# Prompt attention moved beside the end of the attention input projection; sample heads alone in the attention loop, and both prompt output projections at its head

## The chip, the core and the metric

The kernel runs on one core of one Trainium2 chip. That core has TensorE (PE, the matrix multiplies), VectorE (DVE), ScalarE (ACT) and GpSimd (POOL), and SyncE (SP), whose queue issues nearly all transfers between HBM and the on-chip memory. The metric is the device time of one execution in microseconds (us). Everything is computed in float32 precision: each product is built from a rounded high half and a low rest, so that one product takes two or three matmuls.

## The reference

One step of a small diffusion backbone with two layers over 256 prompt tokens and 2048 sample tokens of width 1024. Layer 0 is a convolution branch, layer 1 an attention branch. Only layer 1 matters here:

```
q, k, v, z = split(h @ w_in, 4)                       # 1024 -> 4 x 1024, 16 heads of 64
prompt:  o = softmax(q k^T / 8) v                     # 256 x 256 per head, no mask
sample:  o = softmax([q k_loc^T/8 + bias, q k_ctx^T/8]) [v_loc; v_ctx]
         # k_loc: an 8 x 16 window of the 32 x 64 grid; k_ctx: 512 cached keys
x = x + gate * ((o * silu(z)) @ w_out)                # for prompt and sample, same weights, own gate
y = rms_norm(x) * final_g
```

The outputs are the normalised prompt and sample rows and the new k and v of the prompt. The prompt attention reads nothing that the sample attention makes, and the other way round.

## The kernel before

Phase 1 does the convolution layer and then the projections `w_in` of the attention layer, in two batches: first the prompt and the first 768 sample tokens (list A), later the other 1280 sample tokens (list B). `na_values` makes v, and `na_rest` makes k, z and q in 24 steps, one for each 128 columns of one of the three. A step of list B is 72 matmuls on PE. Every result goes to scratch in HBM (`ks_d`, `qh_d`, `ql_d`, `zn_d`, `vp_d`, `vs_d`), and the attention loads it from there. Instructions of a side list are woven between these steps: `weave(main, side, n)` takes n steps of the side for each step of the main work. The side list beside list B is `context_keys` (8 steps), `masked_bias` (48), `gated_weights` (32; it multiplies `w_out` with the gate and writes it to `w2_d`) and `context_values` (8). The Tile scheduler then sets the order of each engine in phase 1; in phase 2 the written order holds for PE and DVE, and the scheduler orders the other engines.

Phase 2 (`attention`) runs over units. A sample head of a group G of 512 tokens has four units of 128 queries, so 16 heads and 4 groups make 256 units; they come in two half-passes of 8 heads (`hg` 0 and 1, each over G = 0 to 3). One step i of the loop works on several units at once: scores of unit i (`sa_S`), minimum and bias on DVE, exponential on ACT, scaling on POOL, transposes on PE (`sa_T`), splitting in two halves on ACT and DVE (`sa_pt`), and the value product (`sa_O`). Prompt heads are units too: two heads form one unit (`pa_S`, `pa_T`, `pa_O`), and four such units stand at the head of each half-pass as G = None, before its sample heads. In the program text the names of the prompt's loaded tiles are `aNone_k`, `aNone_qh`, `aNone_ql`, `aNone_v` and `aNone_z`.

When a group has its heads done, `out_group` multiplies with half of `w2_d`, in chunks of six matmuls. `side_chunk` runs one chunk in every second step, as filling between the attention's own matmuls; if more than seven tiles would wait (`tiles_left`), `split` runs chunks at once until there is room, a burst. The weights are loaded by `load_w2`: four tiles of 128 x 4 x 512 numbers for one half-pass and one gate, of which the kernel holds one set. The first set is loaded at loop step 18 (`W2_STEP`), each next one as the set before it is finished with. All loads go through SP's queue in order; a load that waits for its buffer holds up all behind it.

```
for hg in range(2):
    ctx = {}
    for G in (None, 0, 1, 2, 3):
        grp = {"hg": hg, "G": G, "n": NPR if G is None else 512}
        self.sequence += [Head(grp, ctx, 8 * hg + i) for i in range(0, 8, 2 if G is None else 1)]
```

Of the kernel before, what the change touches and what calls it, by code (L numbers as in the profile page):

```python
# [11 lines left out]
F32 = mybir.dt.float32  # L12
# [3 lines left out]
ALU = mybir.AluOpType  # L16
# [32 lines left out]
BEGIN = 10  # L49
NEAR = 3  # L50
W2_STEP = 18
# [24 lines left out]
class Kern:  # L76
    def __init__(self, ctx, tc, io):
# [21 lines left out]
        self.rpb_d = d("rpb_d", [P + 1, RPB_PITCH])  # L99

# [941 lines left out]
    def masked_bias(self):  # L1042

        nc = self.nc
        work = lambda shape, tag, bufs, name: self.bp.tile(shape, F32, tag=tag, name=name, bufs=bufs)
# [119 lines left out]

    @staticmethod
    def weave(main, side, n):

        due = 0
        for _ in main:  # L1170
            due += n
            while due >= 1:
                next(side, None)
                due -= 1

    def phase1(self):
        tc = self.tc
        with ExitStack() as c:
# [19 lines left out]
            self.pc = extra.enter_context(tc.tile_pool(name="lnps", bufs=1, space=bass.MemoryType.PSUM))  # L1198
# [11 lines left out]
            side = itertools.chain(self.context_keys(), self.masked_bias(), self.gated_weights(), self.context_values())  # L1210
            rest = self.na_rest(B)
            with tc.tile_pool(name="bp", bufs=1, side="right") as self.bp:
                self.weave(self.na_values(B, lambda: next(rest)), side, 2)
                self.weave(itertools.islice(rest, 21), side, 3.5)
                for _ in side:
                    pass
# [6 lines left out]
    def start_attention(self):  # L1223
# [4 lines left out]
        for hg in range(2):  # L1228
            ctx = {}
            for G in (None, 0, 1, 2, 3):  # L1230
                grp = {"hg": hg, "G": G, "n": NPR if G is None else 512}
                self.sequence += [Head(grp, ctx, 8 * hg + i) for i in range(0, 8, 2 if G is None else 1)]
# [30 lines left out]
    def attention(self):  # L1263
# [3 lines left out]
        units = [(hd, j) for hd in heads for j in ([0] if hd.G is None else range(4))]  # L1267
# [6 lines left out]
        for i in range(-1, len(units) + 4):  # L1274
            self.step = i
            if i == W2_STEP:
                for h in range(2):
                    self.load_w2(0, 0, h, True)

            def go(u, new=False):  # L1280
# [3 lines left out]
                if new:  # L1284
                    if j == 0:
                        self.load_ahead(order[id(hd)] + 1)
                    gens[u] = self.prompt_unit(hd) if hd.G is None else self.sample_unit(hd, j)
# [9 lines left out]
            if 0 <= i - 3 < len(units):  # L1297
                hd, j = units[i - 3]
                if hd.G is None:
                    self.side_chunk()  # L1300
                    self.prompt_values(hd)
                elif j % 2:
# [33 lines left out]
    def load_head(self, hd):  # L1336
        nc, T, h, G, b = self.nc, self.T, hd.h, hd.G, hd.b
        nm = f"a{G}_{h}"
        a = 0 if G is None else NPR + G * 512
        n = hd.n  # L1340
        rows = slice(h // 2 * P, h // 2 * P + P)
        if G is None:
            hd.k = T("kt", [P, 2, NPR], F32R, nm + "_k")
            nc.sync.dma_start(hd.k.bitcast(F32), self.ks_d[h : h + 2, :, :, 0:NPR].rearrange("h s d t -> (s d) h t"))
            hd.q, hd.ql = (T(t, [P, 2, NPR], F32R, f"{nm}_{t}") for t in ("qh", "ql"))
            for t, d in ((hd.q, self.qh_d), (hd.ql, self.ql_d)):
                src = d[h * DH : h * DH + P, 0:NPR].rearrange("(e d) t -> d e t", e=2)
                for half in range(2):
                    nc.sync.dma_start(t[half * DH : half * DH + DH].bitcast(F32), src)
            hd.v = T("vl", [P, 2, 4, DH], F32R, nm + "_v")  # L1350
            nc.sync.dma_start(hd.v.bitcast(F32), self.vp_d[:, h : h + 2].rearrange("(u t) h s d -> t u (h s) d", t=P))
            hd.z = T("z", [P, n], F32, nm + "_z")
            nc.sync.dma_start(hd.z, self.zn_d[rows, a : a + n])
            return
# [42 lines left out]

    def prompt_unit(self, hd):

        nc, T = self.nc, self.T  # L1400
        nm = f"pa{hd.h}"
        S = self.bank("S", nm + "_S", 2, 1024)
        for e in range(2):
            for u in range(2):
                cs = slice(u * P, u * P + P)
                self.scores(S[:, (2 * e + u) * NPR : (2 * e + u + 1) * NPR], hd.q[:, e, cs], hd.ql[:, e, cs], hd.k[:, e])
        yield
        m = self.sm.tile([P, 8], F32, tag="m", name=nm + "_m")
        nc.vector.tensor_reduce(out=m[:, 0:4], in_=S.rearrange("p (x k) -> p x k", x=4), axis=AX.X, op=ALU.min)
        yield  # L1410
        p = T("p", [P, 4, NPR], F32, nm + "_p")
        for x in range(4):
            nc.scalar.activation(p[:, x], S[:, x * NPR : x * NPR + NPR], AF.Exp, scale=-1.0, bias=m[:, x : x + 1], accum_out=m[:, 4 + x : 5 + x])
        nc.vector.reciprocal(m[:, 4:8], m[:, 4:8])
        for x in range(4):
            nc.gpsimd.tensor_scalar(out=p[:, x], in0=p[:, x], scalar1=m[:, 4 + x : 5 + x], scalar2=1.0, op0=ALU.mult, op1=ALU.mult)
        yield
        ts = [self.bank("T", f"{nm}_T{e}", 2) for e in range(2)]
        for e, t in enumerate(ts):
            for u in range(2):  # L1420
                for kc in range(2):
                    nc.tensor.transpose(t[:, (2 * kc + u) * P : (2 * kc + u + 1) * P], p[:, 2 * e + u, kc * P : kc * P + P], self.ident)
        yield
        hd.pt = T("pt", [P, 2, 2, 2, NPR], F32R, nm + "_pt")
        flat = hd.pt.rearrange("p e s k q -> p e s (k q)")
# [289 lines left out]
```

## Time and profile before

| what | value |
|---|---|
| time, median of 3 runs | 2861.8 us (2847.99 to 2865.89) |
| time of the profiled execution | 2854.11 us |
| its span, first to last instruction | 2852.3 us |
| PE busy | 2706.4 us, 95% of the span |
| DVE, ACT, POOL busy | 1847.0, 1439.1, 1505.3 us |
| mean granted TensorE clock | 0.982 |
| DMA | 543.83 MB, mean 191 GB/s |

1.8 us of the profiled time lie outside its span. Times below are counted from the span's start. The last projection of phase 1 ends at about 1804 us and the last attention unit at about 2811 us; what follows is the last group's output projection. A row of the windows view gives a stretch, its length, the busy time of each engine in it with the number of its instructions, the granted clock of TensorE, the busy share of the DMA engines and what they moved. If a line is chosen, the busy time and the count are of that line alone: line L1465 is the reciprocal that each sample unit has once, so its count is the number of sample units in the stretch. L1607 is the third matmul of the output projection; a chunk has two of it. In a row of the timeline stand start, length, engine, line, operation, what is written and read, and in brackets how long the engine stood idle before it and what it waited for.

### The profile page before, as it was taken

How to read it: one execution, taken by the hardware profiler on the slowest of the kernel's cores; microseconds unless marked ns; L12 is line 12 of the kernel's file. 1: busy time of each engine (PE TensorE's matmuls, PEld its weight loads, DVE VectorE, ACT ScalarE, POOL GpSimd, SP SyncE). 2: the span in 40 equal slices, each digit the busy share in tenths (PEclk: the TensorE clock that was granted, in tenths of full speed). 3: DMA queues.
4: the chain of work that ended last, by engine and by line, in shares of the span. 5: the costliest groups of instructions: out<-in, count | busy, mean ns of one | idle time of the engine just before them, and what ended most of it. 6: DMA issues, size and time to landing. Idle time of an engine off the chain costs nothing.

```text
span 2852.3 us, 45385 instructions
## 1 busy us (share of the span) xinstructions
PE 2706.4 (95%) x16079; PEld 2340.2 (82%) x16079; DVE 1847.0 (65%) x3126; ACT 1439.1 (50%) x2538; POOL 1505.3 (53%) x1647
## 2 busy tenths in 40 slices
PE   6999999999899999999999999798999999999998
PEld 4888877776677889999988888687888888888887
DVE  4789989999876500023466530477778776888885
ACT  4457566676543312233222221466667665677774
POOL 4678878888554333355113331344555554556564
PEclk9999999999999999999999999899999999999999
DMA  7233555555435554447789984778776887976763
GB/s 253 87 122 111 190 170 161 185 192 178 148 114 167 161 158 128 121 149 237 238 297 356 339 283 128 195 199 224 202 197 186 212 219 200 248 211 184 199 169 108
DMA packets 429100, 543.83 MB, mean 191 GB/s; under 512 B 42562, under 2 KB 299674, under 8 KB 428745
## 3 DMA queue, kind: packets, MB, share of 16 engines
q1 hardware_dynamic: 423552, 517.97, 60.9%
q10 hardware_dynamic: 5320, 22.95, 2.1%
q8 instruction: 128, 2.10, 0.3%
q14 instruction: 100, 0.81, 0.1%
HBM read 357.76 MB, written 187.13 MB: 191 GB/s over the span
## 4 chain that ended last, share of the span: by engine, by line
PE 73%; DMA 9%; DVE 8%; ACT 4%; POOL 3%; issue 2%; SPq 2%; POOLq 0%; ACTq 0%; DVEq 0%
PE sa_T L1472 7%; PE ni_s L350 6%; PE ni_s L351 6%; PE ni_s L349 6%; PE ci_ps L349 5%; PE ci_ps L350 5%; PE ci_ps L351 5%; PE sa_O L1501 5%; PE sa_O L1496 4%; PE sa_S L1395 3%; PE sa_S L1394 3%; DVE cv L500 2%; PE o L1605 2%; PE o L1607 2%; PE o L1606 2%
## 5 line engine op out<-in xcount | busy, mean ns | idle before, releaser
L1466 POOL TENSOR_SCALAR sa_p<-sa_p,sa_m 128x992 f32<-128x992 f32 (+2 forms) x256 | 279.5, 1092 | 430.4 <-DVE sa_m L1465 307.1
L500 DVE SCALAR_TENSOR_TENSOR cv<-u,dw,cv 128x640 f32<-128x640 f32 (+2 forms) x570 | 427.8, 822 | 3.8 <-ACT cv L496 2.9
L1481 ACT CAST sa_pt<-sa_T 128x512 fp32r<-128x512 f32 (+3 forms) x512 | 275.6, 588 | 228.2 <-PE sa_T L1472 226.5
L109 DVE TENSOR_TENSOR sa_pt<-sa_T,sa_pt 128x512 fp32r<-128x512 f32 (+3 forms) x512 | 328.6, 682 | 3.1 <-ACT sa_pt L1481 2.5
L349 PE MATMUL ci_ps<-h_s_hi,ci_wh 128*128 128x512 f32 x768 | 307.2, 400 | 2.0 <-DVE shift L237 1.0
L351 PE MATMUL ci_ps<-h_s_hi,ci_wl 128*128 128x512 f32 x768 | 303.0, 395 | 0.0
L350 PE MATMUL ci_ps<-h_s_lo,ci_wh 128*128 128x512 f32 x768 | 302.8, 394 | 0.0
L1464 ACT ACTIVATE sa_p<-sa_S,sa_m 128x992 f32<-128x992 f32 (+2 forms) x256 | 267.2, 1044 | 64.4 <-DVE sa_m L1460 52.1
L1472 PE MATMUL sa_T<-ident,sa_p 128*128 128x128 f32 (+3 forms) x2048 | 273.7, 277 | 18.9 <-DVE sa_pt L109 18.4
L1472 PEld LDWEIGHTS sa_T<-ident,sa_p 128*128 128x128 f32 (+3 forms) x2048 | 240.2, 138 | 53.7 <-POOL None_y1l L106 14.2
L1458 DVE TENSOR_REDUCE sa_m<-sa_S 128x1 f32<-128x512 f32 x256 | 176.2, 688 | 161.3 <-PE sa_S L1395 145.0
L481 POOL TENSOR_TENSOR cv_s<-cv_s,cv_p 128x519 f32<-128x519 f32 (+1 forms) x155 | 233.1, 1504 | 69.7 <-DVE cv_s L504 49.0
L478 ACT ACTIVATE cv_p<-u,dw 128x640 f32<-128x640 f32 (+2 forms) x326 | 240.9, 770 | 54.4 <-POOL cv_s L481 35.7
L481 POOL TENSOR_TENSOR cv_p<-cv_p,cv_p 128x520 f32<-128x520 f32 (+1 forms) x155 | 227.7, 1469 | 26.6 <-ACT cv_p L478 18.9
L1501 PE MATMUL sa_O<-sa_pt,a_v 120*128 120x256 f32 (+5 forms) x1280 | 192.6, 281 | 0.0
L1496 PE MATMUL sa_O<-sa_pt,cv 128*128 128x256 f32 x1024 | 177.3, 296 | 2.9 <-ACT sa_pt L1481 1.4
L349 PEld LDWEIGHTS ci_ps<-h_s_hi,ci_wh 128*128 128x128 f32 x768 | 145.2, 189 | 39.1 <-ACT cv_p L478 2.5
L1460 DVE CUSTOM_DVE_ANT_0 sa_S<-sa_S,a_bm,sa_m 128x480 f32<-128x480 f32 (+2 forms) x256 | 170.9, 668 | 9.0
L351 PEld LDWEIGHTS ci_ps<-h_s_hi,ci_wl 128*128 128x128 f32 x768 | 145.1, 189 | 33.8
L350 PEld LDWEIGHTS ci_ps<-h_s_lo,ci_wh 128*128 128x128 f32 x768 | 145.5, 189 | 31.0
L1501 PEld LDWEIGHTS sa_O<-sa_pt,a_v 120*128 120x128 f32 (+2 forms) x1280 | 169.5, 193 | 0.0
L106 POOL TENSOR_TENSOR nis_wl<-nis_w,nis_wh 128x1024 fp32r<-128x1024 f32 x24 | 58.6, 2446 | 187.1 <-ACT nis_wh L341 159.0
(843 smaller groups left out, 7265.1 us busy)
## 6 DMA issues: line engine op xcount, KB each, us to landing
adaw<-in_ada_w SPq DMA_DIRECT2D x24, 1024.0 KB
ci_w<-in_conv_w_in SPq DMA_DIRECT2D x48, 512.0 KB
a_bm<-bm_d SPq DMA_DIRECT2D x32, 720.0 KB
x_s<-in_x_sample SPq DMA_DIRECT2D x32, 512.0 KB
vs_d<-v_s SPq DMA_DIRECT2D x128, 128.0 KB
a_qh<-qh_d SPq DMA_DIRECT2D x128, 128.0 KB
a_ql<-ql_d SPq DMA_DIRECT2D x128, 128.0 KB
o_x<-x_d SPq DMA_DIRECT2D x32, 512.0 KB
```

Of the source, the lines that this page charges most:

```text
L109: self.nc.vector.tensor_tensor(out=lo, in0=src, in1=hi.bitcast(F32), op=ALU.subtract)
L349: self.nc.tensor.matmul(out, wh[:, k, :], hh[:, k, :], start=k == 0, stop=False)
L350: self.nc.tensor.matmul(out, wh[:, k, :], hl[:, k, :], start=False, stop=False)
L351: self.nc.tensor.matmul(out, wl[:, k, :], hh[:, k, :], start=False, stop=k == NK - 1)
L481: nc.gpsimd.tensor_tensor(out=st["sum", half], in0=st["sum", half], in1=st[half, tap], op=ALU.add)
L500: nc.vector.scalar_tensor_tensor(out=out, in0=u, scalar=w, in1=first, op0=ALU.mult, op1=ALU.add)
L1464: nc.scalar.activation(p[:, n], S[:, n], AF.Exp, scale=-1.0, bias=m[:, 2:3], accum_out=m[:, 3:4])
L1466: nc.gpsimd.tensor_scalar(out=p[:, n], in0=p[:, n], scalar1=m[:, 3:4], scalar2=1.0, op0=ALU.mult, op1=ALU.mult)
L1472: nc.tensor.transpose(t[:w, c * P : c * P + P], p[:, x + c * w : x + c * w + w], self.ident)
L1481: nc.scalar.copy(pt[:w, 0, part, :, at], t)
L1496: nc.tensor.matmul(o, cv[:, c].rearrange("p s d -> p (s d)"), x, start=s + c == 0, stop=False)
L1501: nc.tensor.matmul(dst, v[:w, c0 + c].rearrange("p s d -> p (s d)"), loc[:, lo:hi], start=False, stop=s == 1 and c == 3)
```

## The change

The prompt attention leaves the loop of phase 2. A new function, `prompt_attention`, does all eight pairs of heads as a pipeline of seven stages (load, scores, softmax, transposes and split, values, gating, rounding and store), and each pair's gated output goes to a new scratch `yp_d` in HBM. The side work beside list B is now in two parts. `context_keys` and `masked_bias` are woven with `na_values` and the first 13 steps of `na_rest` that follow (3.6 side steps for each); then the memory of the bias tiles is given back and a pool for the prompt is opened in its place; `prompt_attention`, mixed with `gated_weights` and `context_values`, is woven with the next 8 steps (11.5 for each). The last steps of `na_rest` follow without a side. The PSUM banks of the layer norm are freed earlier so that the prompt's scores and outputs have banks.

In phase 2 the sequence holds sample heads alone. At loop step 10 both output projections of the prompt are put in line, `hg` 0 and then `hg` 1; each loads its rounded rows from `yp_d`. An output group that begins with new weights now passes three chunk turns (`WAIT`) instead of one. The first set of `w2` is loaded at loop step 5 instead of 18, and the order of the sets (half-pass, gate) is (0,0), (1,0), (0,1), (1,1), where it was (0,0), (0,1), (1,0), (1,1).

```diff
-W2_STEP = 18
+WAIT = 3
+W2_STEP = 5
@@ phase1
-            side = itertools.chain(self.context_keys(), self.masked_bias(), self.gated_weights(), self.context_values())
...
-                self.weave(self.na_values(B, lambda: next(rest)), side, 2)
-                self.weave(itertools.islice(rest, 21), side, 3.5)
+                with tc.tile_pool(name="mb", bufs=1, side="right") as self.mb:
+                    side = itertools.chain(self.context_keys(), self.masked_bias())
+                    self.weave(self.na_values(B, lambda: next(rest)), side, 2)
+                    self.weave(itertools.islice(rest, 13), side, 3.6)
...
+                with tc.tile_pool(name="pq", bufs=2, side="right") as pq, tc.tile_pool(name="pqs", bufs=1, space=bass.MemoryType.PSUM) as pps:
+                    side = itertools.chain(self.gated_weights(), self.context_values())
+                    side = self.mixed(self.prompt_attention(pq, pps), side, 40 / 52)
+                    self.weave(itertools.islice(rest, 8), side, 11.5)
...
@@ prompt_pair (new): loads of k, q, ql, v, z; then as prompt_unit and prompt_values did; then
+        yh, yl = (T(x, [P, NPR], F32R) for x in ("yh", "yl"))
+        self.round_pool(yh, z)
+        self.rest_pool(yl, z, yh)
+        for s, y in enumerate((yh, yl)):
+            nc.sync.dma_start(self.yp_d[ct, s], y.bitcast(F32))
@@ start_attention
-            for G in (None, 0, 1, 2, 3):
+            for G in range(4):
@@ attention
+            if i == BEGIN:
+                for hg in range(2):
+                    self.chunks.append(self.out_group({"hg": hg, "G": None}))
+                    self.due += 4 * NPR // P + WAIT
+                    self.tiles_left += NPR // P
@@ out_group
+        if G is None:
+            grp["y"] = [tuple(T("y", [P, 4, P], F32R, f"yp{hg}_{u}{s}") for s in "hl") for u in range(NPR // P)]
+            for u, y in enumerate(grp["y"]):
+                for s, t in enumerate(y):
+                    nc.sync.dma_start(t.bitcast(F32), self.yp_d[4 * hg : 4 * hg + 4, s, :, u * P : u * P + P].rearrange("c p t -> p c t"))
         if G is None or G == 0:
-            yield True
+            for _ in range(WAIT):
+                yield True
...
-                    self.load_w2(hg + g, 1 - g, h)
+                    self.load_w2(*{(0, 0): (1, 0), (1, 0): (0, 1), (0, 1): (1, 1), (1, 1): (2, 1)}[hg, g], h)
```

What this does to the order is shown at three places. The first is PE's queue near the end of the attention input projection, where `ni_0` and `ni_3` are the q and z products of column block 4; before, the two products follow each other:

```order
L350 MATMUL ni_0_s_15436<-h_s_hl,nis_4_0_wh 128x256
L351 MATMUL ni_0_s_15436<-h_s_hl,nis_4_0_wl 128x256
L349 MATMUL ni_3_s_15505<-h_s_hi,nis_4_3_wh 128x512
L350 MATMUL ni_3_s_15505<-h_s_lo,nis_4_3_wh 128x512
L351 MATMUL ni_3_s_15505<-h_s_hi,nis_4_3_wl 128x512
```

Now, at the same place, the scores of one pair of prompt heads (`pa_S`) and the transposes of the pair before (`pa_T`) stand between them:

```order
L353 MATMUL ni_0_s_15345<-h_s_hl,nis_4_0_wl 128x256
L1482 MATMUL pa_S<-pa_k,pa_ql 128x256
L1481 MATMUL pa_S<-pa_k,pa_qh 128x256
L1482 MATMUL pa_S<-pa_k,pa_ql 128x256
L1481 MATMUL pa_S<-pa_k,pa_qh 128x256
L1482 MATMUL pa_S<-pa_k,pa_ql 128x256
L1481 MATMUL pa_S<-pa_k,pa_qh 128x256
L1482 MATMUL pa_S<-pa_k,pa_ql 128x256
L1214 MATMUL pa_T_15478<-ident,pa_p 128x128 x4
L1214 MATMUL pa_T_15479<-ident,pa_p 128x128 x4
L351 MATMUL ni_3_s_15499<-h_s_hi,nis_4_3_wh 128x512
```

Each of the eight pairs is put between the projections in this way, over some nine of the last twelve steps; the last two steps (`ni_1` and `ni_0` of block 7) have no prompt work between or behind them.

The second place is PE's queue where the attention loop begins. Before, the first sample units stood between prompt units:

```order
L1439 MATMUL pa_O<-pa_pt,aNone_v 128x256 x8
L1394 MATMUL sa_0_0_S<-ck_16370,a_0_qh 128x512
L1395 MATMUL sa_0_0_S<-ck_16370,a_0_ql 128x512
L1394 MATMUL sa_0_0_S<-a_0_k,a_0_qh 128x352
L1395 MATMUL sa_0_0_S<-a_0_k,a_0_ql 128x352
L1422 MATMUL pa_T_16874<-ident,pa_p 128x128 x4
L1422 MATMUL pa_T_16875<-ident,pa_p 128x128 x4
L1439 MATMUL pa_O<-pa_pt,aNone_v 128x256 x8
L1394 MATMUL sa_0_1_S<-ck_16370,a_0_qh 128x512
```

Now they stand alone, behind the last projection:

```order
L353 MATMUL ni_0_s_17218<-h_s_hl,nis_7_0_wl 128x256
L1481 MATMUL sa_0_0_S<-ck_16930,a_0_qh 128x512
L1482 MATMUL sa_0_0_S<-ck_16930,a_0_ql 128x512
L1481 MATMUL sa_0_0_S<-a_0_k,a_0_qh 128x352
L1482 MATMUL sa_0_0_S<-a_0_k,a_0_ql 128x352
L1481 MATMUL sa_0_1_S<-ck_16930,a_0_qh 128x512
L1482 MATMUL sa_0_1_S<-ck_16930,a_0_ql 128x512
```

The third place is SP's queue at the loads of the fourth sample head (`a_3`). Before, they came ahead of the first weights, and the set of weights came three heads later:

```order
L1367 DMA a_4_ql<-ql_d 64x512 x2
L1567 DMA w2h_17480<-w_d 128x4x512
L1567 DMA w2l_17481<-w_d 128x4x512
L1567 DMA w2h_17486<-w_d 128x4x512
L1567 DMA w2l_17487<-w_d 128x4x512
L1370 DMA a_7_z<-zn_d 128x512
```

Now the weights stand ahead of the fourth head's loads:

```order
L1467 DMA ck_18307<-kc_d 128x512
L1600 DMA w2h_17397<-w_d 128x4x512
L1600 DMA w2l_17398<-w_d 128x4x512
L1600 DMA w2h_17403<-w_d 128x4x512
L1600 DMA w2l_17404<-w_d 128x4x512
L1469 DMA cv_18309<-cvs_d 128x4x128
L1477 DMA a_3_v<-vs_d 88x8x128
L1454 DMA a_3_qh<-qh_d 64x512
```

The weights have moved from behind the loads of the fifth head to ahead of those of the fourth, and two more sets follow in the same half-pass, where it was one.

More of the change, by code (lines that the diff above doesn't have):

```diff
@@ L99, in __init__ @@
         self.rpb_d = d("rpb_d", [P + 1, RPB_PITCH])
+        self.yp_d = d("yp_d", [NK, 2, P, NPR])
     def round_pool(self, out, src):
@@ L1044, in masked_bias @@
         nc = self.nc
-        work = lambda shape, tag, bufs, name: self.bp.tile(shape, F32, tag=tag, name=name, bufs=bufs)
+        work = lambda shape, tag, bufs, name: self.mb.tile(shape, F32, tag=tag, name=name, bufs=bufs)
         masks = [work([P, 3, 480], "mask", 3, f"mask{gk}") for gk in range(3)]
@@ L1166, in weave, with mixed @@
+    @staticmethod
+    def mixed(a, b, n):
+        due = 0
+        for _ in a:
+            yield
+            due += n
+            while due >= 1:
+                due -= 1
+                if next(b, FAR) is not FAR:
+                    yield
+        yield from b
     @staticmethod
@@ L1197, in phase1 @@
             self.xp = extra.enter_context(tc.tile_pool(name="extra", bufs=1))
[L1198 removed]
+            norms = extra.enter_context(ExitStack())
+            self.pc = norms.enter_context(tc.tile_pool(name="lnps", bufs=1, space=bass.MemoryType.PSUM))
             A, B = [], []
@@ L1229, in start_attention @@
             ctx = {}
-            for G in (None, 0, 1, 2, 3):
-                grp = {"hg": hg, "G": G, "n": NPR if G is None else 512}
-                self.sequence += [Head(grp, ctx, 8 * hg + i) for i in range(0, 8, 2 if G is None else 1)]
+            for G in range(4):
+                grp = {"hg": hg, "G": G, "n": 512}
+                self.sequence += [Head(grp, ctx, 8 * hg + i) for i in range(8)]
         self.loaded = 0
@@ L1266, in attention @@
         heads = self.sequence
-        units = [(hd, j) for hd in heads for j in ([0] if hd.G is None else range(4))]
+        units = [(hd, j) for hd in heads for j in range(4)]
         self.late = {}
@@ L1298, in attention @@
                 hd, j = units[i - 3]
[L1299 to L1302, printed above, removed]
+                if j % 2:
                     rest = self.sample_values(hd, j // 2)
@@ L1338, in load_head @@
         nm = f"a{G}_{h}"
-        a = 0 if G is None else NPR + G * 512
+        a = NPR + G * 512
         n = hd.n
         rows = slice(h // 2 * P, h // 2 * P + P)
[L1342 to L1354, printed above, removed]
         r0, R = KEY_ROWS[G]
@@ L1395, in scores @@
         self.nc.tensor.matmul(out, ql, k, start=False, stop=True)
[L1398 to L1425, printed above, removed]
-        for e, t in enumerate(ts):
-            nc.scalar.copy(flat[:, e, 0], t)
-            self.rest_dve(flat[:, e, 1], t, flat[:, e, 0])
-    def prompt_values(self, hd):
-        o = self.bank("mm" if hd.h % 4 and not self.chunks else "O", f"pa{hd.h}_O", 1)
-        both = [Head(hd.grp, hd.ctx, hd.h + e) for e in range(2)]
-        for e, one in enumerate(both):
-            one.o, one.z = o[:, e * NPR : e * NPR + NPR], hd.z
-            for s in range(2):
-                for kc in range(2):
-                    v = hd.v[:, kc, 2 * e : 2 * e + 2].rearrange("p s d -> p (s d)")
-                    self.nc.tensor.matmul(one.o, v, hd.pt[:, e, s, kc], start=s + kc == 0, stop=s + kc == 2)
-        for one in both:
-            self.head_out(one)
     def sample_unit(self, hd, j):
@@ L1522, in gate @@
         def gate():
-            if hd.G is None:
-                nc.vector.tensor_tensor(out=sz, in0=of, in1=sz, op=ALU.mult)
-                return
             zv = sz.rearrange("p (r j c) -> p j r c", j=4, c=16)
@@ L1543, in split @@
             if ct % 4 == 3 and u == nt - 1:
-                def begin():
-                    self.chunks.append(self.out_group(grp))
-                    self.due += 4 * nt + (hd.G is None or hd.G == 0)
-                if hd.G is None and grp["hg"] == 0:
-                    self.put_off(BEGIN, begin)
-                else:
-                    begin()
+                self.chunks.append(self.out_group(grp))
+                self.due += 4 * nt + (WAIT if hd.G == 0 else 0)
         self.put_off(2, gate)
```

73 lines of the change are left out of this document (70 added, 3 removed).

## The prediction

> **What bounds the kernel now.** I read the page first, then the stretches of the attention loop by the windows view, then the waits and the timeline where a stretch is longer than its neighbours. The page says that PE is the engine to watch:
>
> ```profile
> PE 2706.4 (95%) x16079; PEld 2340.2 (82%) x16079; DVE 1847.0 (65%) x3126; ACT 1439.1 (50%) x2538; POOL 1505.3 (53%) x1647
> ```
>
> The change removes no matmul, so what it can gain is time in which PE is idle or its clock low. To find that time I cut the loop at sample units. These are the windows with the reciprocals of line L1465 counted, one for each unit; the first row is the stretch from the last projection to the first unit.
>
> ```profile
> 1804.40:1824.90 20.50, 0.00 (x0) 0.83 0.80 216
> 1824.90:1950.60 125.70, 5.23 (x32) 0.92 0.83 219
> 1950.60:2078.10 127.50, 5.25 (x32) 0.96 0.80 208
> 2078.10:2195.50 117.40, 5.24 (x32) 1.00 0.72 195
> 2195.50:2295.60 100.10, 4.59 (x28) 1.00 0.79 205
> 2295.60:2333.40 37.80, 0.66 (x4) 0.86 0.80 217
> 2333.40:2462.90 129.50, 5.25 (x32) 0.99 0.78 204
> ```
>
> The same windows with line L1607, from the first unit on, give the output projection's chunks, half of each count: 7, 15, 16, 14, 4 and 21.
>
> ```profile
> 1824.90:1950.60 125.70, 5.49 (x14) 2.62 (x14) 0.92 0.83 219
> 1950.60:2078.10 127.50, 11.82 (x30) 5.63 (x30) 0.96 0.80 208
> 2078.10:2195.50 117.40, 12.63 (x32) 6.00 (x32) 1.00 0.72 195
> 2195.50:2295.60 100.10, 11.00 (x28) 5.25 (x28) 1.00 0.79 205
> 2295.60:2333.40 37.80, 3.63 (x8) 1.78 (x8) 0.86 0.80 217
> 2333.40:2462.90 129.50, 16.49 (x42) 7.88 (x42) 0.99 0.78 204
> ```
>
> Two stretches are quiet, at clock 1.00: group 2 with 117.4 us for 32 units, and group 3 with 100.1 / 28 = 3.575 us a unit, which is 114.4 us for 32. A head without chunks takes less:
>
> ```profile
> 1876.90:1889.10 12.20, 0.65 (x4) 1.00 0.83 286
> ```
>
> That is 3.05 us a unit, so a chunk in group 3 costs (100.1 - 28 x 3.05) / 14 = 1.05 us. By these rates the first group lost 125.7 - 97.6 - 7 x 1.05 = 20.8 us, group 1 lost 127.5 - 117.4 + 1.05 = 11.2, the four units with the second prompt block 37.8 - 12.2 - 4.2 = 21.4, and the next group 129.5 - 97.6 - 22.0 = 9.9. These 63 us and the 20.5 us of the first row are what the change touches.
>
> In the first group one loss stands by itself: DVE, with the sample heads behind it, waits for a prompt tile that came late through SP's queue.
>
> ```profile
> 1850.13 0.42 DVE L1524 TENSOR_TENSOR aNone_z<-None_of,aNone_z 128x256 f32<-128x256 f32 x1 [9.85 <-DMA aNone_z<-zn_d]
> ```
>
> The remaining 20.8 - 9.85 = 10.9 us fall where the first set of output weights is loaded, and group 1's 11.2 us where the second is. There PE waits for q tiles (all of them between 1790 and 2060 us), and its clock is low behind it:
>
> ```profile
> PE sa_S L1395 <- DMA a_ql<-ql_d: 9.6, 4, 3.3
> 1980.00:1990.00 10.00, 8.24 (x43) 7.65 (x44) 3.89 (x8) 2.84 (x6) 1.09 (x1) 0.66 1.04 215
> ```
>
> The last row is a window of all engines; 0.66 is the granted clock, 1.04 the DMA share. After the second prompt block two sets are loaded, and 9.9 us are lost: 5.0 for a set.
>
> **The change part by part.** *The prompt's matmuls.* PE in the timeline, at the first prompt block:
>
> ```profile
> 1804.21 0.27 PE L351 MATMUL ni_s<-h_s_hl,nis_wl 128*128 128x256 f32 x1
> ...
> 1811.79 0.55 PE L1394 MATMUL pa_S<-aNone_k,aNone_qh 128*128 128x256 f32 x1 [4.58 <-DMA aNone_qh<-qh_d]
> 1812.74 0.55 PE L1395 MATMUL pa_S<-aNone_k,aNone_ql 128*128 128x256 f32 x1 [0.40 <-DMA aNone_ql<-ql_d]
> ...
> 1819.26 0.47 PE L1394 MATMUL sa_S<-ck,a_qh 128*128 128x512 f32 x1
> 1820.27 0.47 PE L1395 MATMUL sa_S<-ck,a_ql 128*128 128x512 f32 x1 [0.54 <-DMA a_ql<-ql_d]
> ...
> 1820.92 1.10 PE L1422 MATMUL pa_T<-ident,pa_p 128*128 128x128 f32 x8
> 1821.78 1.19 PE L1439 MATMUL pa_O<-pa_pt,aNone_v 128*128 128x256 f32 x8
> 1822.80 0.40 PE L1394 MATMUL sa_S<-ck,a_qh 128*128 128x512 f32 x1
> 1824.34 1.22 PE L1422 MATMUL pa_T<-ident,pa_p 128*128 128x128 f32 x8 [0.55 <-POOL pa_p L1416]
> ```
>
> From start to start the eight transposes take 0.86 us and the eight value matmuls 1.02; the eight score matmuls have the same shape, so 1.02 again: 2.9 us a pair, 23.2 us for eight. In phase 1 this is added in full, because PE has no gap there to take it in:
>
> ```profile
> 1700.00:1750.00 50.00, 50.00 (x266) 43.25 (x265) 1.81 (x3) 9.12 (x15) 15.93 (x13) 1.00 0.73 214
> 1750.00:1800.00 50.00, 50.00 (x255) 42.77 (x254) 1.81 (x3) 5.82 (x12) 5.41 (x5) 1.00 0.24 71
> ```
>
> The columns are PE, PEld, DVE, ACT, POOL, clock, DMA share and GB/s. What the prompt asks of DVE, ACT and POOL is covered, since DVE is at 4% there, ACT under 20%, POOL at a third or less; if that cover were gone, PE would wait as for `pa_p` above, 0.55 us. Its DMAs count as well:
>
> ```profile
> aNone_k<-ks_d SPq DMA_DIRECT2D x8, 256.0 KB
> aNone_qh<-qh_d SPq DMA_DIRECT2D x16, 128.0 KB
> aNone_ql<-ql_d SPq DMA_DIRECT2D x16, 128.0 KB
> aNone_v<-vp_d SPq DMA_DIRECT2D x8, 256.0 KB
> ...
> aNone_z<-zn_d SPq DMA_DIRECT2D x8, 128.0 KB
> ```
>
> A pair loads 1.15 MB and now also stores its rows, 0.26 MB: 11 MB in all, against 71 and 214 GB/s in stretches of a kernel that reaches 286 above. Bandwidth is there. On SP these loads go between the projections' stores and the next weights; each pair has two buffers, so a load has two steps of projection, some 27 us (a step is 72 matmuls, and the rows above have 266 in 50 us), before PE needs it. **Phase-1 waits** lie between nothing and 8 x (4.58 + 0.40) = 40 us; below nothing isn't possible, as PE is full. I take 3 us, near the lower end: only the first pair's loads are close, since their pool opens when the last bias tiles are stored.
>
> *The loop's start.* Before, 20.5 us. Now the first unit's chain has no other work beside it. In the rows above unit 0 takes 5.6 us from its first score to its reciprocal at 1824.9, 0.54 of it a wait for a load: I take 5.0. The start is then 23.2 + 3 + 5.0 = 31.2 us, **10.7 us more**. Sample loads of the first two heads are behind the last prompt store on SP, with two projection steps to land in.
>
> *The body to unit 160.* From there on the order of both is the same. To that point both do 80 chunks, so the new one costs, at the quiet rates, three times 114.4 (groups 0, 3 and 0 again) and twice 117.4 (1 and 2): 578.0 us. The old one took 638.0.
>
> *Weights.* They stay four sets, but three now load in the first half-pass, on top of the context keys of new heads, and one in the second. DVE holds the first load at step 5 by four tiny copies; behind them stand the minima of unit 5, but the memory they wait for is free once phase 1 has ended. On SP the set now stands ahead of the fourth head's q, k and bias, and PE waits for those. By the rows a set costs 5.0 us (second half-pass) to 11 us (first). Four sets cost 20 us at the least rate and 3 x 11 + 5 = 38 at the greatest; nothing at all if the halves, spread out now, find room. I take 28, midway, since the later sets are loaded in halves, four units apart, as the set that cost 11.2 was too, but with shorter key tiles beside them for one of the two.
>
> On the clock: the row 1980 to 1990 loses 10 x 0.34 = 3.4 us beyond its waits. The Trainium skill (TensorE: Matmul & The Clock Gate, Part 1: The HAM clock gate) states that an idle window of about 3.4 us halves the clock until one busy window has passed, which as an estimate is 1.7 us for each such stall. The trace has twice that here. By the page the four sets would cost about 7 us less, and the sum would end at some 2836; that lies within the forecast's own case and gets no chance apart, and I go by the row. The same rule speaks against the new start, where nothing covers the first chain; there the row of 5.6 us has the low clock in it already.
>
> *Bursts.* Five chunks at once (units 13 and 45) instead of three, with PE waiting for the one bank; I add 3 us, the price of three chunks that now fill no gap; at least nothing, at most 6.
>
> **Sum:** body 578.0 + 28 + 3 = 609.0 against 638.0, that is -29.0; start +10.7; together **-18.3 us**. The profiled execution, 2854.1 us, would be 2835.8. The runs shown have a median of 2861.8, 7.7 above it, so I put the same difference there: **2843 us**. A difference under 1% (28.6 us) can't be told from no change here.
>
> **The rivals.**
>
> *The weights are hidden (2815).* Each half set has some ten units to land in. At 286 GB/s against the 208 that the heads take, 2.1 MB need 27 us, and ten units give 36. Then the 28 us go: -46. For it speaks that the fourth set alone lost little; against it, that q loads queue behind the weights on SP whatever the mean rate, and that group 1 had spread halves as well.
>
> *No change (2862).* The sample heads starve at the start: context keys, `yp_d` rows, residual rows and the first weights all come in the first 15 units, and twice something as late as the prompt's z (9.85 us) holds the loop. +20 takes the gain away. For it: the row of 9.85 arose in this way, through one queue. Against: without the prompt units, four pairs of loads fewer stand in it.
>
> *Slower (2903).* PE runs strictly in order, so each pair in phase 1 can stop the projections. If every pair met the waits of the first block in the open, 4.58 + 0.40 + 0.55 and again 0.55 for the values, that is 6.1 us, and its clock loss of 3.4 in every second pair, eight would cost 62 us instead of 3: +59 - 18. It decides from (18.3 + 3) / 8 = 2.7 us a pair. For it: SP's queue is in order and holds stores that wait for POOL and ACT. Against: DMA share 0.24 and 0.73 in the rows above.
>
> That the move does not take place is excluded: the order of PE shows the prompt between the projections.
>
> **Numbers.** Forecast 0.5, hidden weights 0.2, no change 0.15, slower 0.15. The range takes in -18.3 - 28 - 3 = 2812.5 at the low end, and at the high end 38 us for the weights with a part of the phase-1 bound: 2843 + 10 + 28 = 2881. Faster by over 1% means under 2833: the hidden weights and a quarter of the forecast, 0.33. Slower by over 1% means over 2890: most of the last rival, 0.12. Within 1%: 0.55.
>
> **What would show it.** Phase 1: PE full from 1650 us on and the last projection some 23 to 26 us later than 1804; waits of `pa_S` on a DMA there speak for the slow rival. Start: five to six us from the last projection to the first reciprocal. Loop: the four units at the second half-pass fall from 37.8 to some 14 us; groups 0 and 1 take 114 to 128 us each; waits of `sa_S` for q near the three sets add to 13 to 30 us with their clock. The prediction is wrong if the first group takes over 140 us, or if groups 0 and 1 run at the quiet rate.

## The result, and the profile after

The changed kernel takes 2841.35 us (median of 10 runs, 2837.14 to 2847.02) against 2858.82 us (10 runs, 2846.7 to 2865.89) for the kernel before: a ratio of 0.9947, 95% interval 0.993 to 0.9964. By this ratio it is 15.2 us less, with an interval from 10.3 to 20.0 (the two medians lie 17.5 apart). That is under 1%, which the prediction couldn't tell from no change; with so narrow an interval it can be told. Forecast were 2843 us and -18.3.

The profiled execution of the changed kernel took 2847.02 us, 5.7 above its median, and that of before 2854.1, 4.7 below its own; so the two traces differ by 7 us only. I therefore read beside it a second profile of the same kernel, from the run c1_changed below (2838.79 us, near its median of 2840.59). PE's load has hardly moved:

```profile
PE 2702.7 (95%) x16079; PEld 2339.1 (82%) x16079; DVE 1848.0 (65%) x3126; ACT 1448.6 (51%) x2544; POOL 1507.1 (53%) x1631
```

The windows view of the changed kernel, cut at the same units as before. The columns are the window, its length, DVE's busy time and count for the reciprocals of the sample units (now line L1507), the granted clock, the DMA share and GB/s. The first row is the start, from the last projection to the first unit; then come groups 0, 1 and 2, the first 28 units of group 3, the four units at the second half-pass, and the groups of the second half-pass.

```profile
1837.20:1842.90 5.70, 0.00 (x0) 1.00 0.49 153
1842.90:1974.40 131.50, 5.24 (x32) 0.92 0.89 244
1974.40:2101.00 126.60, 5.25 (x32) 0.99 0.80 224
2101.00:2218.40 117.40, 5.24 (x32) 1.00 0.72 197
2218.40:2318.30 99.90, 4.59 (x28) 1.00 0.76 205
2318.30:2331.90 13.60, 0.66 (x4) 1.00 0.81 221
2331.90:2444.40 112.50, 5.25 (x32) 1.00 0.75 187
2444.40:2571.10 126.70, 5.24 (x32) 0.99 0.77 213
2571.10:2692.00 120.90, 5.26 (x32) 0.99 0.69 190
```

The same of the kernel before for the last two, which the prediction did not show, and of the second profile of the changed kernel for its start, its group 0, the four units, and the second group of its second half-pass:

```profile
2462.90:2582.10 119.20, 5.24 (x32) 1.00 0.82 232
2582.10:2700.30 118.20, 5.25 (x32) 1.00 0.69 194
```

```profile
1829.30:1834.90 5.60, 0.00 (x0) 1.00 0.46 134
1834.90:1966.70 131.80, 5.23 (x32) 0.91 0.89 243
2310.60:2324.20 13.60, 0.65 (x4) 1.00 0.80 212
2436.70:2566.10 129.40, 5.24 (x32) 0.97 0.74 208
```

The four units with the second prompt block went from 37.8 to 13.6 us, the start from 20.5 to 5.7, and the first group of the second half-pass from 129.5 to 112.5. Against that, the last projection ends at 1837.2 (in the second profile at 1829.3) instead of 1804.4, group 0 takes 5.8 us more, and the second group of the second half-pass 7.5 to 10.2 us more.

In phase 1 PE is still full, with more matmuls in the same time, until the last step. The windows view of all engines (PE, PEld, DVE, ACT, POOL, clock, DMA share, GB/s), and the one wait of PE over 1 us between 1640 and 1840:

```profile
1700.00:1750.00 50.00, 50.00 (x294) 44.26 (x294) 15.32 (x27) 23.15 (x53) 24.85 (x28) 1.00 0.77 236
1750.00:1800.00 50.00, 50.00 (x294) 44.26 (x293) 12.08 (x23) 18.91 (x43) 20.78 (x25) 1.00 0.39 126
1820.00:1830.00 10.00, 2.92 (x7) 2.34 (x8) 0.42 (x1) 0.97 (x2) 1.79 (x2) 0.69 0.86 223
PE ni_s L351 <- DVE ni_s_l L111: 7.1, 1, 7.1
```

No score of a prompt pair waits for a load. The one wait has another origin. In the program text the start of the attention stands ahead of the last projection steps in both kernels, but SP's order differs. In the kernel before, the last `zn_d` stores of the gate were issued long ahead of the first attention loads:

```profile
1755.49 22.15 SPq L1004 DMA_DIRECT2D zn_d<-ni_s_f  x6
1806.17 0.63 SPq L1349 DMA_DIRECT2D aNone_qh<-qh_d  x1
```

Now SP issues the loads of the first heads from 1797.7 us on, and the last `zn_d` stores behind them. The cast of the next keys waits for the buffer that this store frees, and PE for the bank that the cast and DVE's step behind it free. The timeline of the changed kernel (start, length, engine; in brackets the idle time before it and what ended it):

```profile
1818.51 2.40 SPq L1006 DMA_DIRECT2D zn_d<-ni_s_f  x2
1826.14 0.37 ACT L1101 CAST ni_s_h<-ni_s 128x256 fp32r<-128x256 f32 x1 [13.80 <-DMA zn_d<-ni_s_f]
1827.08 0.80 PE L351 MATMUL ni_s<-h_s_hi,nis_wh 128*128 128x512 f32 x1 [7.15 <-DVE ni_s_l L111]
```

In group 0 the loss stands where the prediction put the first set of weights. SP issues the set from 1857.97 on; the fourth head's q comes behind it, and its issue takes 3.85 us instead of about half a microsecond:

```profile
1857.97 0.56 SPq L1600 DMA_DIRECT2D w2h<-w_d  x1
1869.58 3.85 SPq L1454 DMA_DIRECT2D a_qh<-qh_d  x1
1884.52 0.76 PE L1481 MATMUL sa_S<-ck,a_qh 128*128 128x512 f32 x1 [11.29 <-DMA a_qh<-qh_d]
1888.11 0.77 PE L1482 MATMUL sa_S<-ck,a_ql 128*128 128x512 f32 x1 [2.83 <-DMA a_ql<-ql_d]
```

The waits view of PE on q, between 1840 and 1976 us (first two rows: total, times, longest) and between 2444 and 2640 (third row; the kernel before has none there):

```profile
PE sa_S L1481 <- DMA a_qh<-qh_d: 11.3, 1, 11.3
PE sa_S L1482 <- DMA a_ql<-ql_d: 8.0, 3, 3.6
PE sa_S L1482 <- DMA a_ql<-ql_d: 5.4, 2, 3.6
```

### The profile page after: what moved, and what is told of

Same layout as the page of the kernel before. It is cut to its first block, busy times and chain, and to the rows that moved or that the text cites. A ratio compares the mean times of both kernels' runs of the same rounds, so it can differ in the third digit from the quotient of the medians.

```text
span 2845.2 us, 45399 instructions
## 1 busy us (share of the span) xinstructions
PE 2702.7 (95%) x16079; PEld 2339.1 (82%) x16079; DVE 1848.0 (65%) x3126; ACT 1448.6 (51%) x2544; POOL 1507.1 (53%) x1631
## 5 line engine op out<-in xcount | busy, mean ns | idle before, releaser
L351 PE MATMUL ni_s<-h_s_hi,nis_wh 128*128 128x512 f32 x384 | 152.2, 396 | 12.4 <-DVE ni_s_l L111 8.7
```

Source lines behind the costliest of these rows:

```text
L351: self.nc.tensor.matmul(out, wh[:, k, :], hh[:, k, :], start=k == 0, stop=False)
```

## The experiments

Each ratio is to the kernel before, timed beside it on the same chip; one per mille is 2.9 us.

**The changed kernel again** (no edit).

> The changed kernel itself once more, as the reference for the others on the same chip. Theory: 0.9947 of the kernel before (0.993 to 0.9964), so 13 to 20 us faster. In its profile PE should again wait some 7 us in the last projections (behind DVE's split of a k tile, L111) and some 11 to 14 us at the scores of the fourth sample head (q loads). Rival: both waits belong to one execution and are under 3 us here.

2840.59 us, ratio 0.9946 (0.9931 to 0.9962). The two waits are there again, with 5.8 us in phase 1 and 10.7 for the fourth head's q. They belong to the program, not to one execution. What does change between executions lies ahead of the edit: the 1,728 matmuls of the last projections begin at 1463.2 here, at 1467.9 in the first profile, and at 1466.0 in before.

**The start of the attention one step later**, so that the last `zn_d` store is issued ahead of the first heads' loads.

```diff
+            next(rest)
             extra.close()
             self.start_attention()
```

> The first heads' loads are issued one projection step later in the program, so that SP has the last z stores ahead of them. Theory: in the changed kernel the z stores stood behind 17 loads, so their buffers came free late and PE waited 7.1 us; this wait goes, with its low clock: 7 to 10 us faster than the changed kernel, ratio to before 0.991 to 0.9925. Rival: the first unit then waits for its loads as long, the start is 5 to 10 us longer, and the ratio stays at 0.994 to 0.996.

2840.35 us, ratio 0.9947 (0.9932 to 0.9961): no gain. Yet the edit did what it should. The longest wait of PE in phase 1 that is left, and then group 0, which took 131.8 us in the second profile:

```profile
PE ni_s L351 <- ACT ni_s_f L1013: 1.2, 1, 1.2
```

```profile
1835.30:1971.80 136.50, 34.36 (x65) 0.89 0.88 241
```

(The second row is the window of the units of group 0; its busy column belongs to another line here.) The 1,728 matmuls took 5.2 us less, and group 0 took 4.7 more, with a wait for the fourth head's q of 12.6 instead of 10.7. So the time that phase 1 saves is lost again in the loop, in the first 24 units, of which each eight take 1.3 to 1.9 us more. Why they do is not shown.

**The first weight set at step 8 instead of 5**, behind the fourth head's loads.

```diff
-W2_STEP = 5
+W2_STEP = 8
```

> The first set of output weights is loaded at loop step 8 instead of 5, which puts it behind the fourth head's loads on SP. Theory (the order in the queue counts): the wait of 11.3 + 2.8 us at the fourth head falls under 4 us, the burst five units later waits for the weights at most 4 us, and the kernel is 6 to 12 us faster than the changed one, ratio 0.990 to 0.9925. Rival (the rate counts): the same bytes pass in the same time, the wait goes to the burst or to the fifth head, and the time is within 3 us of the changed kernel.

2831.18 us, ratio 0.9916 (0.9903 to 0.993): about 9 us less than the changed kernel, and the place on SP's queue is shown to be a cause: SP issues the fourth head's q 17.7 us behind the first unit's reciprocal, where it was 26.7 in the second profile, and PE begins that head at 30.2 instead of 41.0. Group 0, and what is left of PE's waits on q in it:

```profile
1835.10:1956.50 121.40, 5.24 (x32) 0.93 0.95 265
PE sa_S L1482 <- DMA a_ql<-ql_d: 7.8, 2, 7.7
```

Units 8 to 16 fall from 48.8 to 34.0 us, units 16 to 24 rise from 31.5 to 37.3: the head after the set waits now, but once.

**Both edits together.**

> Both edits together: loads one projection step later, first weights at step 8. Theory: the two waits are apart and add, 13 to 22 us faster than the changed kernel, ratio 0.987 to 0.990. Rival: one wait takes the other's place, and it is no better than the better of the two alone.

2832.78 us, ratio 0.992 (0.9908 to 0.9932), the same as the later set alone. The later start again gains nothing. In the profile group 0 takes 129.3 us here and 121.4 with the later set alone; but this profile is 5 us above the median of its kernel, so part of that may be chance.

**Every prompt score, transpose and value matmul of phase 1 done twice**, with the same result.

```diff
-    self.scores(S[...], q[:, e, cs], ql[:, e, cs], k[:, e])
+    for _ in range(2):
+        self.scores(S[...], q[:, e, cs], ql[:, e, cs], k[:, e])
...
-    for kc in range(2):
+    for kc in (0, 0, 1, 1):
...
-    for e in range(2):
+    for e in (0, 0, 1, 1):
```

> The changed kernel with every matmul and transpose of the prompt attention done twice (same result), 192 more on PE in phase 1. Theory: PE is full there, so they are added in full: 8 pairs x 2.9 us = 23 us slower than the changed kernel (21 to 26), the last projection as much later, ratio to before 1.001 to 1.004. Rival 1 (PE has room there): under 10 us slower. Rival 2 (each pair stops the projections by its waits): the extra work hides in those waits, also under 10 us.

2859.92 us, ratio 1.0018 (1.0008 to 1.0029): 7.2 per mille, 20.6 us, more than the changed kernel. In the trace the 1,728 matmuls and what stands between them take 27.8 us more, 2.7 of it in the wait on the `ni_s_l` bank (8.5 us instead of 5.8). A second prompt costs 25.1 us by the trace and 20.6 by the times; 23.2 was the term.

**One prompt output projection in each half-pass**, with the old order of the sets; the attention of the prompt stays in phase 1.

```diff
-            if i == BEGIN:
-                for hg in range(2):
+            if i % (len(units) // 2) == BEGIN and i < len(units):
+                for hg in (2 * i // len(units),):
...
-    self.load_w2(*{(0, 0): (1, 0), (1, 0): (0, 1), (0, 1): (1, 1), (1, 1): (2, 1)}[hg, g], h)
+    self.load_w2(hg + g, 1 - g, h)
```

> The prompt attention stays in phase 1, but the prompt's output projection of the second half-pass goes back to that half-pass, and the weight sets go back to their old order, two in each half-pass. Theory: the gain comes from the prompt blocks that left the loop, and four sets cost about the same in either order: within 8 us of the changed kernel, ratio 0.992 to 0.997; groups 0 and 1 of the first half-pass some 8 us shorter, the second half-pass as much longer. Rival: putting both projections first carries the gain, 10 us or more slower, ratio 0.998 or more.

2848.79 us, ratio 0.9965 (0.9952 to 0.9978), some 5 us more than the changed kernel; the two intervals overlap. The losses change places: group 0 takes 120.0 us instead of 131.8, and the first group of the second half-pass 129.8 instead of 112.5. Most of the gain stays without the new order, so it comes from the prompt's attention in phase 1; the order of the output projections and sets is worth about a third of it by the ratios, which is not clear of noise. The longer pause before a group with new weights (`WAIT`) was not tested by itself.

**Only the first weight set loaded.** The other three are left out and the first is used in their place, so the outputs behind them are not the reference's.

```diff
+        if not hold:
+            self.w2.setdefault((hg, g), []).append(self.w2[0, 0][h])
+            return
```

> Leaves out the loads of the second, third and fourth set of output weights; the first set is used for all four. Theory: later sets cost by their place, 2.7 us for the second, 7 to 9 each for the third and fourth: 14 to 22 us faster than the changed kernel, ratio 0.987 to 0.990, with the first set's wait of 11 to 14 us unchanged. Rival (weights hidden): under 5 us faster, ratio 0.993 or more.

2824.33 us, ratio 0.9882 (0.9867 to 0.9897): 18 us less, so the weights aren't hidden. The windows of groups 0 and 1 and of the second group of the second half-pass tell which sets:

```profile
1837.00:1962.80 125.80, 5.24 (x32) 0.92 0.82 222
1962.80:2089.40 126.60, 5.26 (x32) 0.99 0.69 191
2434.40:2555.30 120.90, 5.26 (x32) 1.00 0.69 189
```

Against the second profile (131.8, 126.5, 129.4) the second set costs 6.0 us and the third, for which 7 to 9 were expected, nothing; the fourth costs 8.5, and 0.9 in the group behind it. Such prices from two profiles are good to some 3 us: group 0 takes 128.9 us in the run with the doubled prompt, whose loop is the same, and the fourth set's group 126.7 in the first profile. What group 1 loses against group 2 (117.4) stays there without the third set, so it is not the weights. About 3 us of it are its three more chunks, 19 against 16. Most of the rest lies in units 40 to 48, at the burst of chunks ahead of unit 45, where DVE has nothing to do for 6 us, in this same kernel (all engines):

```profile
2014.00:2020.00 6.00, 4.32 (x19) 3.07 (x18) 0.00 (x0) 1.17 (x2) 3.99 (x5) 1.00 0.21 69
```

Five chunks stand there in a row, because the first y of a new group may be written only when no more than 7 tiles are left with its own four, with 14 y buffers.

**All weights issued on ACT's queue instead of SP's.**

```diff
-            self.nc.sync.dma_start(w[s].bitcast(F32), ...)
+            self.nc.scalar.dma_start(w[s].bitcast(F32), ...)
```

> Changed kernel, but all four sets of output weights are issued on ACT's queue instead of SP's. Theory of the queue's order: the q tiles no longer stand behind 4 MB on SP, so the wait of sa_S for qh at the fourth head (10.7 to 11.3 us) falls under 3 us, units 8 to 16 fall from 48.5 to 34 to 38 us, and the time is 8 to 20 us under the changed kernel's 2841 (ratio 0.988 to 0.992). Rival, the transfers themselves: the same bytes share the DMA engines in the same stretch, q is as late as before, ratio 0.9946 within 0.002. Second rival: ACT is held by its own issue and waits, seen as waits of sa_T or sa_O on ACT of over 5 us in all, and the time is over 2841.

2830.8 us, ratio 0.9909 (0.9894 to 0.9924), some 10 us less than the changed kernel. The 10.7 us wait for q is gone (2.1 us remain on `a_ql` in group 0). But this run doesn't show that the queue's order made that wait, since the mechanism of the second rival is there too, though not its time of over 2841. ACT's timeline while the set is issued:

```profile
1849.51 0.19 ACT L1506 ACTIVATION_READ_ACCUMULATOR sa_p<-sa_S,sa_m 128x1 f32 x1
1853.90 0.41 ACTq L1600 DMA_DIRECT2D w2h<-w_d  x1
1858.25 2.03 ACTq L1600 DMA_DIRECT2D w2l<-w_d  x1
1860.32 1.06 ACT L1523 CAST sa_pt<-sa_T 128x512 fp32r<-128x512 f32 x2 [10.62 <-issue]
```

ACT does nothing else for 10.6 us, and units 0 to 8 take 34.2 us instead of 23.1. So PE comes to the fourth head no earlier. The first unit's reciprocal starts at 1839.0 us here and at 1835.0 in the second profile; SP issues that head's q 28.2 us behind it here and 26.7 there, and PE begins the head 41.2 us behind it here and 41.0 there (the first row is of this run, the second of the second profile):

```profile
1880.23 0.48 PE L1481 MATMUL sa_S<-ck,a_qh 128*128 128x512 f32 x1
1875.96 0.77 PE L1481 MATMUL sa_S<-ck,a_qh 128*128 128x512 f32 x1 [10.68 <-DMA a_qh<-qh_d]
```

The wait has changed its place, from q to ACT. That the order on SP's queue is a cause is shown by the later set above, not by this run. Of the gain, 3.3 us lie in units 0 to 16, 6.1 in units 16 to 32, where the second set is loaded, and 4.9 in the second group of the second half-pass, that of the fourth set (124.5 us instead of 129.4).

**Sixteen y buffers and a limit of 8 tiles**, paid for with one residual buffer.

```diff
-"y": 14, "x": 3
+"y": 16, "x": 2
...
-while self.tiles_left + nt > 7:
+while self.tiles_left + nt > 8:
```

> Changed kernel with 16 instead of 14 y buffers and a limit of 8 instead of 7 tiles that may be left when a group's first y is written; two instead of three residual buffers pay for it. Theory that the bursts of five chunks cost 3.3 us (unit 13), 6.9 (unit 45) and 3.1 (unit 173): they shrink to one chunk, units 40 to 48 fall from 39.8 to 33 us, the time is 6 to 12 us under 2841 (ratio 0.990 to 0.9925). Rival: the chunks cost the same wherever they stand, or the two residual buffers make them wait; ratio 0.9946 within 0.002, units 40 to 48 over 38.

2823.74 us, ratio 0.9887 (0.9872 to 0.9902): 17 us less, more than expected. Units 40 to 48 take 32.5 us instead of 39.8 (with fewer chunks, 4.7 instead of 6.7). The windows of groups 0, 1 and 2 and of two groups of the second half-pass:

```profile
1840.10:1965.70 125.60, 5.24 (x32) 0.90 0.91 250
1965.70:2091.30 125.60, 5.26 (x32) 0.97 0.76 214
2091.30:2209.20 117.90, 5.25 (x32) 1.00 0.71 201
2433.20:2557.00 123.80, 5.25 (x32) 0.97 0.79 217
2557.00:2673.20 116.20, 5.25 (x32) 1.00 0.74 204
```

Most of it comes in the two groups where a prompt's chunks or a set of weights meet the burst: 6.2 and 5.6 us. The others gain between nothing and three. In group 1 itself 0.9 us are gained, though the burst is gone from units 40 to 48: units 48 to 56 take 34.9 us instead of 29.0, with a wait for q of 3.4 that the changed kernel doesn't have there. The edit changes y buffers, limit and residual buffers at once; no run takes them apart.

**The wider y and the later set.**

> The wider y and the first weight set held until unit 8 together. If the burst and the place of the set are separate costs, their gains add: 9 and 6 to 12 us under 2841, that is 2820 to 2826 (ratio 0.987 to 0.989). If they are the same time seen twice, 2831 (0.9916) as with the later set alone.

2815.23 us, ratio 0.9856 (0.9839 to 0.9873). The two gains, 3.0 and 5.9 per mille, add to 0.9857 from 0.9946: two separate costs. This version is the fastest here, 40 us under the kernel before.

**ACT's queue and the later set.**

> Weights on ACT's queue and the first set held until unit 8. Theory of the queue's order: at unit 8 the fourth head's loads were ahead anyway, so for the first set ACT's queue adds little; what it adds is the fourth set (9.5 us) and the second (6): 2818 to 2826 (ratio 0.986 to 0.989). Rival, the transfers themselves: 2831 (0.9916) as with the later set alone.

2827.63 us, ratio 0.9901 (0.9888 to 0.9915). It lies between what the two theories gave and tells nothing apart; PE has a wait of 7.0 us for ACT's `sa_p` in group 0, so ACT is still held there.

**The wider y in the kernel before.**

> The kernel before, not the changed one, with the wider y of e8 (16 y buffers, limit 8, two residual buffers). e8 took 17 us from the changed kernel. If the cost of the bursts belongs to the change (both prompt projections first, so that four of its tiles are left when the first sample group ends, against two before), the kernel before gains little: within 6 us of its own time, ratio 0.998 to 1.001. If the bursts at every group's end cost this in both kernels, before gains 12 to 18 us, ratio 0.9937 to 0.9958, and the term for bursts in the prediction was right to be small.

2845.11 us, ratio 0.9959 (0.9942 to 0.9975): 11.7 us less than before, just under what the second theory gave. So the kernel before gains from the same edit too, by more than half as much. What the change adds is 16.9 - 11.7 = 5 us, with an interval of about 8 either way.

## Why the prediction was right

The balance, from the second profile of the changed kernel against that of before; all times are cut at the last projection and at units 0 and 160:

| step | predicted, us | measured, us |
|---|---|---|
| last projections with the prompt between them | +26.2 (23.2 + 3) | +27.6 |
| start, 5.0 against 20.5 | -15.5 | -14.8 |
| units 0 to 160 | -29.0 | -36.2 |
| behind unit 160 | 0 | +11.3 |
| together | -18.3 | -12.1 |
| by the timed runs | -18.3 | -15.2 |

The two spans differ by 15.3 us. What the table doesn't hold of that, 3.2, lies outside the edit: 2.8 ahead of it, where the second profile's last projections began earlier than before's, and 0.4 behind the last unit. In the first profile they began 1.9 us later, and took 30.8 us more than before's with a wait of 7.1.

**The prompt's matmuls: right.** They were added in full: 27.6 less the wait of 5.8 is 21.8 us, 23.7 in the first profile, 25.1 and 20.6 by the doubling; the term was 23.2. DVE, ACT and POOL had room: in the fullest of the two quoted windows POOL is busy for half of it.

**Phase-1 waits: 3 us taken, 5.8 to 7.1 measured, and not where I looked.** I costed the loads of the prompt pairs, and those never came late. I named SP's stores as a danger only in the rival. The wait came from moving the first heads' loads ahead of the last gate store on the same queue, a move that I had read only from the side of the loads ("two projection steps to land in"). The later start shows that these microseconds can't simply be taken back: without the wait the kernel is no faster, and group 0 is longer.

**The start: right**, 5.7 us against 5.0. The low clock that the prediction feared there did not come: the granted clock is 1.00 in the row of the new start. Nor was it in the row of 5.6 us, as the prediction says: from 1819.2 to 1824.9 us the kernel before has 1.00.

**The body to unit 160: the four units right, the rest better.** 13.6 us against "some 14". Groups 0 and 1, at 131.5 and 126.6, did not run at the quiet rate, and stayed under the 140 that I had set as the mark of failure; group 0 is outside the 114 to 128 that I gave. Its reason is the wait behind the first set that the prediction named: units 8 to 16 take 14.8 us more than with the set behind the head's loads. A small error helped: the sum took 80 chunks up to unit 160 for both, but its own counts add to 77, and the changed kernel does 78, at 1.05 us each some 2 us less.

**"From there on the order of both is the same": wrong.** Both kernels load their fourth set about unit 160 (2463.0 us in the kernel before, 2436.8 in the second profile), but not in the same order. Before, each half of it was issued behind the low half of a head's q (`a_ql`); now each stands ahead of one, whose issue takes 3.7 to 4.3 us, and PE waits. The first half in the kernel before, and then in the second profile with the first wait:

```profile
2458.78 1.09 SPq L1367 DMA_DIRECT2D a_ql<-ql_d  x2
2465.90 0.38 SPq L1567 DMA_DIRECT2D w2h<-w_d  x1
```

```profile
2433.39 0.42 SPq L1600 DMA_DIRECT2D w2h<-w_d  x1
2434.56 3.74 SPq L1454 DMA_DIRECT2D a_ql<-ql_d  x2
2449.91 0.50 PE L1482 MATMUL sa_S<-ck,a_ql 128*128 128x512 f32 x1 [2.39 <-DMA a_ql<-ql_d]
```

PE waits for q 5.4 us there in the first profile and 6.4 in the second, where before had no wait. Without this set the two groups behind unit 160 are 9.4 us shorter; that its place in the queue is what costs is read from the rows and not tested. The set was in the sum, but ahead of unit 160: units 0 to 160 came out better than predicted by 7.2 us, and what follows worse by 11.3.

**The weights: 28 us taken, some 27 by the timed runs**, 9 for the place of the first set and 18 for the three others. The first set was moved and never left out, so what it costs in its new place is not in this. By the profiles the parts are 10.4 in group 0 for the first set (131.8 to 121.4), then 6.0, nothing, and 9.4. The total came out right with parts that the prediction didn't have, and that is partly luck. The prediction divided the 9.9 us of one group by two sets, but the kernel before issues the fourth set from 2465.9 us on, behind that group, so one set stands in it; at 9.9 to 11 us a set, four would have been put at 40 to 44. And not all of the 11.2 in group 1 were weights: with the wider y that group of the kernel before takes 123.3 us instead of 127.5. In the changed kernel the first set was the dearest, and one set was hidden altogether. "The weights are hidden" (2815) falls with the run that leaves three sets out; a part of it was true for the third set.

**Bursts: 3 us taken, 5 measured**, with an interval that excludes neither nothing nor 12. That the wider y takes 12 us from the kernel before already was not seen: in the prediction the quiet rate has the bursts in it, as chunks of 1.05 us, and the profile shows only that DVE is idle there.

**The clock.** Behind the second of the fourth head's two waits for q the second profile's timeline has

```profile
1880.23 0.76 PE L1482 MATMUL sa_S<-ck,a_ql 128*128 128x512 f32 x1 [3.51 <-DMA a_ql<-ql_d]
1885.83 0.39 PE L1481 MATMUL sa_S<-ck,a_qh 128*128 128x512 f32 x1
```

The same matmul takes 0.76 us when the wait ends and 0.39 us some 5.6 us later. So at most 5.6 us ran at half speed, a loss of at most 2.8. The Trainium skill (TensorE: Matmul & The Clock Gate, Part 1: The HAM clock gate) gives about 3.4 us of work at half rate, as an estimate a loss of 1.7; the trace agrees within what it can resolve. The prediction's 3.4 us for a stall, read from the mean clock of a 10 us window, was too much: that mean has idle time in it, in which a low clock costs nothing (PE is busy for 8.24 of the 10 us).

**The forecast's 2843 against 2841.35** is closer than its parts deserve, and that is luck. The difference was predicted 3 us too large (18.3 against 15.2), inside its interval, and the median of three runs that it started from, 2861.8, was 3 us above that of ten, 2858.8; the two errors cancel, as do those on either side of unit 160. The rivals "no change" and "slower" fall: 0.9964 is the upper end of the interval, and no score of a prompt pair waited for a load.

## What to carry to other kernels

A large load should be issued behind the small ones of the next work, not only early enough by bandwidth: three steps of delay for one set were worth 9 us, without a byte less. When work is moved past a place where loads are issued, look at the stores that now stand behind those loads, since they free buffers that someone waits for; but taking such a wait away need not make a kernel faster, as the later start shows. When a wait disappears, look whether its engine only came there later for another reason. And work that a limit of buffers forces into a run of its own can cost like a stall, though PE is busy for most of it: two more y buffers, with one more tile allowed and one residual buffer less, were worth 17 us here, as much as the change itself.

## What the runs showed of the hardware

The issue of a DMA can be dear. SP's issue of one q tile took 3.85 us behind a weight set; in the same trace, at 1882 us, a load of the same size took 0.44. When ACT issued the first set, it did nothing else for 10.6 us; the records of the four issues add up to 3.2 us of that, and what filled the rest the profile doesn't show. The Trainium skill (DMA: Bandwidth & Descriptors, Issuing engines are not separate DMA queues) states that all issuing engines share the same 16 DMA engines, and that a second one saves only the time on the sequencer that it takes to initiate a DMA, which is usually small beside the DMA itself. By that page's rule the move to ACT would have been worth next to nothing; it measured 10 us, most of it at the second and the fourth set. At the first set the time only went from PE's wait for q to ACT, at a DMA share as full as before (1.06 between 1850 and 1862 us and 1.08 in the 11 us behind; 1.05 and 1.10 in the second profile). What holds the issue, the runs don't show.
